# A Strassen up-projection, with the gated channels and an embedding product through DRAM, in a one-core transformer layer

## The chip, the core and the metric

The kernel runs on one core of a Trainium2 chip. The metric is the device time of one execution in microseconds (us): the median of three runs.

## What is computed

One decoder layer on 512 tokens of width 2048, all in 32-bit floats: input norm and projection, two groups of mixing heads, an output projection, and then the part that the change touches:

```python
h = h + rms_norm(mixed, ln_mix_post[l])
y = conv_gated_mlp(rms_norm(h, ln_ffn_pre[l]), w_up[l], conv_w[l], conv_b[l], w_down[l])
h = h + rms_norm(y, ln_ffn_post[l])
h = h + (p[l] @ w_pe[l]) * jax.nn.sigmoid(h @ w_pg[l])

def conv_gated_mlp(u, w_up, conv_w, conv_b, w_down):
    up = u @ w_up
    pad = jnp.pad(up, ((0, 0), (CONV_WIDTH - 1, 0), (0, 0)))
    up = conv_b + sum(pad[:, j:j + S] * conv_w[j] for j in range(CONV_WIDTH))
    gate, val = jnp.split(up, 2, axis=-1)
    return (jax.nn.gelu(gate, approximate=True) * val) @ w_down
```

w_up is 2048 x 11264 (5632 gate and 5632 value channels), w_down 5632 x 2048, w_pg 2048 x 2048, w_pe 256 x 2048; the convolution has three taps along the tokens.

## The kernel before, in words

**Matmuls.** Each 32-bit operand is split exactly into two parts of a shorter float type, a high part `hi` (a cast on ScalarE, ACT) and a low part `lo` (a subtraction on VectorE, DVE), and a product is three matmuls: hi by hi, hi by the activations' low part, lo by hi. The inner dimension of 2048 is 16 blocks (`kb`) of 128. `project_cols` (lines 148 to 150) has the weights stationary and gives channels by tokens; `project_rows` (lines 165 to 167) has the activations stationary and gives tokens by columns. Weights come as 1-MB loads that SyncE (SP) issues into two tiles `raw` (line 120), and are split in halves of 128x1024 (lines 132 and 133) into four `hi` and four `lo` tiles, which each come free when the matmuls that read them have ended. The same split of activations is lines 178 and 179 (`split_to`).

**Order.** A scheduler of the framework fixes the order of every engine's instructions when the program is built; pieces of code have priorities (`PRI_W` for weights, `PRI_E` for evictions), and generators in a list `steps` are run a step at a time between the matmuls. Nothing is reordered when the program runs: an instruction that waits holds up all that stand behind it on its engine or DMA queue.

**Stages.** After the mixing heads and the output projection (`ps_wo`), `residual` (lines 645 to 684) takes two of the four 128-token tiles at a time: x is loaded in 256-KB pieces `xp` on ACT's queue through two tiles (line 652), added (653), the result `y` is squared and summed for the norm (657, 658), written to `h_dram` from GpSimd's queue (POOL, 660), scaled (667), transposed on TensorE (PE, 679) and split into the activations u2T. While the second half of the tokens goes through this, the first 256 channels of gate and of value are projected for the first half of the tokens (`ps_ue`, matmuls of 256 columns).

Then the MLP runs over 22 pairs of channel blocks of 128. `up_gate` (736) projects a pair of gate blocks with matmuls of 512 tokens (`ps_ug`), `up_val` (747) the value blocks (`ps_uv`). The convolution is an ACT instruction with scale and bias (726) and two DVE instructions (727, 728); gelu is 743, gate by value 755, and the product is split into gT. After every second pair, `down` (767) multiplies the four blocks of gT before with 512 rows of w_down (`ps_dn`) and adds into `yacc` (763, 765). The last two groups of four blocks (`ps_dl`) are left for the tail, where the norm and residual (`finish`, 786 to 806), the transposes of h (815), the gate product (`ps_pg`) and the embedding product of p (`ps_pe`) follow, and `gate_out` (855 to 858) writes the output.

## Time and profile before

| | us |
|---|---|
| runs | 2604.68 median (2603.14 to 2606.24) |
| profiled execution | span 2600.5, from the first to the last instruction |
| PE busy | 2560.4 (98%) |
| DVE busy | 1255.1 (48%) |
| ACT busy | 903.0 (35%) |
| POOL busy | 118.0 (5%) |
| mean granted clock of PE | 0.998 of full speed |

Of the profiled execution the span alone is known; the runs' median is 4.2 us above it. A row of the profile has its line in the kernel, engine, operation, and output<-inputs by the names in the code, without buffer numbers. Matmuls overlap, so the distance between starts tells what one costs.

### The profile page before, as it was taken

The numbers are of one execution on the slowest core, as the hardware profiler recorded it, in microseconds if no ns is written. First come the engines' busy times: TensorE is split into PE (matmuls) and PEld (weight loads), VectorE is DVE, ScalarE is ACT, GpSimd is POOL, SyncE is SP. The second block draws the span as 40 slices with busy tenths as digits, with TensorE's granted clock in tenths as the row PEclk, the third lists the DMA queues.
The fourth block names the chain that finished last, engine by engine and source line by source line (L and its number), as shares of the span: only waits on it lengthen the run. The fifth ranks groups of instructions, "written<-read, shape, count | busy, mean of one in ns | idle before, by whom it ended". The sixth has DMA issues, their size and how long they took to land.

```text
span 2600.5 us, 28630 instructions
## 1 busy us (share of the span) xinstructions
PE 2560.4 (98%) x11821; PEld 2131.2 (82%) x11821; DVE 1255.1 (48%) x1772; ACT 903.0 (35%) x1244; POOL 118.0 (5%) x123
## 2 busy tenths in 40 slices
PE   7999999999999999999999999999999999999999
PEld 6888888888888788888888888888888888887787
DVE  5467377344453674244444444444444444368533
ACT  4454355233343553332323232323232323344321
POOL 1101011000000000000000000000000000004000
PEclk9999999999999999999999999999999999999999
DMA  5222222322343763332223222222222232256522
GB/s 198 87 86 80 89 85 86 110 90 89 98 146 118 242 207 113 98 98 97 97 97 98 97 97 97 98 97 97 98 98 97 97 97 97 97 197 191 170 97 81
DMA packets 211550, 293.36 MB, mean 113 GB/s; under 512 B 5612, under 2 KB 141788, under 8 KB 210396
## 3 DMA queue, kind: packets, MB, share of 16 engines
q1 hardware_dynamic: 206460, 276.33, 32.4%
q0 software_dynamic: 2656, 11.01, 1.1%
q10 hardware_dynamic: 2304, 4.20, 0.5%
q8 instruction: 93, 1.52, 0.2%
q14 instruction: 37, 0.30, 0.0%
HBM read 279.45 MB, written 12.06 MB: 112 GB/s over the span
## 4 chain that ended last, share of the span: by engine, by line
PE 93%; DMA 3%; DVE 2%; ACT 1%; issue 1%; POOL 0%; SPq 0%; ACTq 0%; POOLq 0%; DVEq 0%
PE ps_ug L150 6%; PE ps_uv L149 6%; PE ps_uv L150 6%; PE ps_ug L149 6%; PE ps_ug L148 6%; PE ps_uv L148 6%; PE ps_dn L165 5%; PE ps_dn L166 5%; PE ps_dn L167 5%; PE ps_pg L165 2%; PE ps_pg L166 2%; PE ps_pg L167 2%; PE ps_wo L165 2%; PE ps_wo L166 2%; PE ps_wo L167 2%; PE ps_hf L148 1%
## 5 line engine op out<-in xcount | busy, mean ns | idle before, releaser
L150 PE MATMUL ps_uv<-u2T,lo_uv 128*128 128x512 f32 x672 | 261.6, 389 | 0.0
L149 PE MATMUL ps_uv<-u2T,hi_uv 128*128 128x512 f32 x672 | 261.6, 389 | 0.0
L148 PE MATMUL ps_ug<-u2T,hi_ug 128*128 128x512 f32 x672 | 261.6, 389 | 0.0
L148 PE MATMUL ps_uv<-u2T,hi_uv 128*128 128x512 f32 x672 | 261.6, 389 | 0.0
L150 PE MATMUL ps_ug<-u2T,lo_ug 128*128 128x512 f32 x672 | 261.6, 389 | 0.0
L149 PE MATMUL ps_ug<-u2T,hi_ug 128*128 128x512 f32 x672 | 261.6, 389 | 0.0
L133 DVE TENSOR_TENSOR lo_ug<-raw_ug,hi_ug 128x1024 fp32r<-128x1024 f32 x88 | 107.8, 1225 | 244.9 <-ACT hi_ug L132 244.8
L165 PE MATMUL ps_dn<-hi_dn,gT 128*128 128x512 f32 x576 | 224.2, 389 | 0.0
L167 PE MATMUL ps_dn<-hi_dn,gT 128*128 128x512 f32 x576 | 224.2, 389 | 0.0
L166 PE MATMUL ps_dn<-lo_dn,gT 128*128 128x512 f32 x576 | 224.2, 389 | 0.0
L133 DVE TENSOR_TENSOR lo_uv<-raw_uv,hi_uv 128x1024 fp32r<-128x1024 f32 x88 | 107.8, 1225 | 217.8 <-ACT hi_uv L132 217.7
L132 ACT CAST hi_uv<-raw_uv 128x1024 fp32r<-128x1024 f32 x88 | 92.4, 1050 | 259.5 <-PE ps_dn L167 149.7
L132 ACT CAST hi_ug<-raw_ug 128x1024 fp32r<-128x1024 f32 x88 | 92.6, 1054 | 256.2 <-PE ps_uv L149 252.0
L133 DVE TENSOR_TENSOR lo_dn<-raw_dn,hi_dn 128x1024 fp32r<-128x1024 f32 x72 | 88.2, 1225 | 168.8 <-ACT hi_dn L132 168.8
L149 PEld LDWEIGHTS ps_ug<-u2T,hi_ug 128*128 128x128 f32 x672 | 126.2, 188 | 26.1
L148 PEld LDWEIGHTS ps_uv<-u2T,hi_uv 128*128 128x128 f32 x672 | 126.2, 188 | 26.2
L149 PEld LDWEIGHTS ps_uv<-u2T,hi_uv 128*128 128x128 f32 x672 | 126.2, 188 | 26.1
L148 PEld LDWEIGHTS ps_ug<-u2T,hi_ug 128*128 128x128 f32 x672 | 126.2, 188 | 26.1
L150 PEld LDWEIGHTS ps_ug<-u2T,lo_ug 128*128 128x128 f32 x672 | 126.2, 188 | 26.1
L150 PEld LDWEIGHTS ps_uv<-u2T,lo_uv 128*128 128x128 f32 x672 | 126.2, 188 | 26.1
L132 ACT CAST hi_dn<-raw_dn 128x1024 fp32r<-128x1024 f32 x72 | 75.6, 1050 | 195.9 <-PE ps_dn L167 117.2
L167 PEld LDWEIGHTS ps_dn<-hi_dn,gT 128*128 128x128 f32 x576 | 108.2, 188 | 22.5
(315 smaller groups left out, 5250.4 us busy)
## 6 DMA issues: line engine op xcount, KB each, us to landing
raw_ug<-in_w_up SPq DMA_DIRECT2D x44, 1024.0 KB, 5.0
raw_uv<-in_w_up SPq DMA_DIRECT2D x44, 1024.0 KB, 5.0
raw_dn<-in_w_down SPq DMA_DIRECT2D x36, 1024.0 KB, 5.0
raw_wo<-in_w_out SPq DMA_DIRECT2D x24, 1024.0 KB, 5.1
raw_pg<-in_w_pg SPq DMA_DIRECT2D x20, 1024.0 KB, 5.3
raw_dl<-in_w_down SPq DMA_DIRECT2D x16, 1024.0 KB, 5.1
raw_hi<-in_w_in SPq DMA_DIRECT2D x8, 1024.0 KB, 5.7
raw_hq<-in_w_in SPq DMA_DIRECT2D x8, 1024.0 KB, 5.1
```

The costliest lines, as they stand in the source:

```text
L132: nc.scalar.copy(hi, raw[:, k0 : k0 + step, :])
L133: nc.vector.tensor_tensor(lo, raw[:, k0 : k0 + step, :], hi.bitcast(F32), op=ALU.subtract)
L148: nc.tensor.matmul(o, hi[:, i, cols], ah, start=kb == 0, stop=False)
L149: nc.tensor.matmul(o, hi[:, i, cols], al, start=False, stop=False)
L150: nc.tensor.matmul(o, lo[:, i, cols], ah, start=False, stop=kb == KB - 1)
L165: nc.tensor.matmul(ps[t], ah[:, cols], hi[:, i, :], start=kb == 0, stop=False)
L166: nc.tensor.matmul(ps[t], ah[:, cols], lo[:, i, :], start=False, stop=False)
L167: nc.tensor.matmul(ps[t], al[:, cols], hi[:, i, :], start=False, stop=kb == nkb - 1)
```

## The change

The up-projection is done block by block of 128 gate and 128 value channels, 44 in all. The inner dimension is halved (8 blocks of 128), the tokens are halved (256) and gate and value are the two halves of the channels: a product of 2 x 2 by 2 x 2 blocks, which seven products of sums of halves give in place of eight. `ua[1]` to `ua[7]` are the sums of activation halves, made once; the sums of weight halves (lines 798, 799, 800, 804) are made for each block, and each operand is split (`split_pair`, ACT line 638, DVE line 639). A product is 24 matmuls of 256 columns (813 to 815). Three PSUM tiles per block collect the products; copies on ACT (820, 855) and additions on DVE (835, 846, 852) take the partial results between products. Convolution, gelu and product are lines 863 to 869, and the gated block is written to `g_dram` by POOL (870). Weights come as four 512-KB loads per block (783), whose rows have 512 bytes, into tiles of `rawp` and, for odd blocks, of the MLP's own pool `ml`.

The embedding product of p moves from the tail to the place between output projection and MLP; its 16 tiles of 128x512 `pv` are copied by ACT (765) into the two tiles that `xp` also uses and written to `pe_dram` by POOL (766); `gate_out` loads them again (992). The write of h_dram is issued by ACT (687). The down-projection follows when all blocks are done: gated blocks are loaded from g_dram (901), split, and multiplied in three parts of 24, 12 and 8 blocks. Its pool `fin` takes the memory of `ml`, so the loads of `lno_b` (893) and of the first gated blocks wait for ml's last reader, the last write to g_dram. Tiles for squares that nobody reads become bfloat16, and the scratch of GpSimd's DMAs is set to 8192.

```diff
+    g_dram = tc.dram_tile([NFB, P, S], F32, name="g_dram")
+    pe_dram = tc.dram_tile([S, D], F32, name="pe_dram")
...
+    def split_pair(pool, src, ncol, name):
+        hi = splitp.tile([P, H8, ncol], F32R, tag="hi", name=f"hi_{name}")
+        lo = splitp.tile([P, H8, ncol], F32R, tag="lo", name=f"lo_{name}")
+        nc.scalar.copy(hi, src)
+        nc.vector.tensor_tensor(lo, src, hi.bitcast(F32), op=ALU.subtract)
+        return hi, lo
...
+        def turn_half(src, dst, t, name):
+            for c in range(2):
+                ps = aux.tile([P, 4, P], F32, tag="aux", name=f"{name}{c}")
+                for i in range(4):
+                    nc.tensor.transpose(ps[:, i, :], src[:, (c * 4 + i) * P : (c * 4 + i + 1) * P], ident)
+                r = slice(c * 4, c * 4 + 4)
+                split_to(dst[:, r, 0, half[t % 2]], dst[:, r, 1, half[t % 2]], ps)
...
+                nc.scalar.dma_start(h_dram[t * P : (t + 1) * P, :], y[t])
                 nc.vector.tensor_reduce(st[t][:, 2:3], sq[t][:, 4:8], axis=mybir.AxisListType.X, op=ALU.add)
                 power(st[t][:, 3:4], st[t][:, 2:3], 1, D)
-                nc.gpsimd.dma_start(h_dram[t * P : (t + 1) * P, :], y[t])
...
+        def second_half():
+            yield from residual((2, 3))
+            for t in (2, 3):
+                scale(t, (2, 3, 0, 1))
+            for t in (2, 3):
+                turn_half(y[t][:, k2], ua[3], t, f"u3t{t}")
+                nc.vector.tensor_tensor(y[t - 2][:, k1], y[t - 2][:, k1], y[t][:, k1], op=ALU.subtract)
+                nc.vector.tensor_tensor(y[t][:, k1], y[t][:, k2], y[t][:, k1], op=ALU.subtract)
+                turn_half(y[t - 2][:, k1], ua[5], t, f"u5t{t}")
+                nc.vector.scalar_tensor_tensor(
+                    y[t][:, k2], y[t - 2][:, k1], -1.0, y[t][:, k2], op0=ALU.mult, op1=ALU.subtract
+                )
+                turn_half(y[t][:, k2], ua[6], t, f"u6t{t}")
+                nc.vector.scalar_tensor_tensor(
+                    y[t - 2][:, k2], y[t][:, k2], -1.0, y[t - 2][:, k2], op0=ALU.mult, op1=ALU.subtract
+                )
+                yield
...
+            for t in (2, 3):
+                turn_half(y[t][:, k1], ua[7], t, f"u7t{t}")
+            for t in (2, 3):
+                turn_half(y[t - 2][:, k2], ua[4], t, f"u4t{t}")
...
-        steps.append(residual((2, 3)))
+        pT = act_slot("A1", "pT")
...
+        p_act = slot_view([pT], 4)
+        for n in range(4):
+            pe = project_rows(w_pe[0], 0, n * S, 2, p_act, full, acc, f"pe{n}", unit=2)
+            for t in range(TT):
+                with tc.high_priority(PRI_E):
+                    pv = wo.tile([P, S], F32, tag="xp", bufs=2, name=f"pv{t}_{n}")
+                    nc.scalar.copy(pv, pe[t])
+                    nc.gpsimd.dma_start(pe_dram[t * P : (t + 1) * P, cut[n]], pv)
+        ua[3], ua[5] = b_slot(0, "ua3", 256), b_slot(1, "ua5", 256)
+        ua[6], ua[7] = act_slot("A0", "ua6", 256), act_slot("A1", "ua7", 256)
+        ua[4] = a4p.tile([P, H8, 2, 256], F32R, name="ua4")
+        steps.append(second_half())
...
-        early = {}
-        for c0 in (0, DFF):
-            early[c0] = project_cols(
-                w_up[0], c0, 2, slot_view(u2T, 4), acc, f"ue{c0}", tok=slice(0, 2 * P),
-                pri=PRI_W if c0 == 0 else 1,
-            )
...
+        def load_group(j):
+            raws = []
+            for k in range(2):
+                r = (ml if j % 2 else rawp).tile([P, H8, 2, P], F32, tag="raw", bufs=2, name=f"raw_u{j}_{k}")
+                for i, c in enumerate((j * P, DFF + j * P)):
+                    nc.sync.dma_start(
+                        r[:, :, i, :],
+                        w_up[0, k * H8 * P : (k + 1) * H8 * P, c : c + P].rearrange("(k p) n -> p k n", p=P),
+                    )
+                raws.append(r)
+            return raws
...
+        def operands(j):
+            r1, r2 = load_group(j)
+            w11, w12, w21, w22 = r1[:, :, 0, :], r1[:, :, 1, :], r2[:, :, 0, :], r2[:, :, 1, :]
+            s5 = ml.tile([P, H8, P], F32, tag="s5", name=f"s5_{j}")
+            ops = {}
+            with tc.high_priority(PRI_W):
+                ops[1] = split_pair(ml, w11, P, f"u{j}_1")
+                ops[2] = split_pair(ml, w21, P, f"u{j}_2")
+                nc.vector.tensor_tensor(s5, w12, w22, op=ALU.add)
+                nc.vector.tensor_tensor(w12, w11, w12, op=ALU.add)
+                nc.vector.tensor_tensor(w11, s5, w11, op=ALU.add)
+                ops[6] = split_pair(ml, w11, P, f"u{j}_6")
+                ops[5] = split_pair(ml, s5, P, f"u{j}_5")
+                ops[7] = split_pair(ml, w12, P, f"u{j}_7")
+                nc.vector.tensor_tensor(w21, w21, w11, op=ALU.add)
+                ops[3] = split_pair(ml, w21, P, f"u{j}_3")
+                ops[4] = split_pair(ml, w22, P, f"u{j}_4")
+            return ops
...
+        def product(o, ops, i, first):
+            hi, lo = ops[i]
+            for kb in range(H8):
+                ah, al = ua[i][:, kb, 0, :], ua[i][:, kb, 1, :]
+                nc.tensor.matmul(o, hi[:, kb, :], ah, start=first and kb == 0, stop=False, skip_group_check=True)
+                nc.tensor.matmul(o, hi[:, kb, :], al, start=False, stop=False, skip_group_check=True)
+                nc.tensor.matmul(o, lo[:, kb, :], ah, start=False, stop=kb == H8 - 1, skip_group_check=True)
...
+            def begin(self):
+                product(self.a, self.ops, 1, True)
+                self.x = partial(self.a, f"xx{self.j}")
+                product(self.b, self.ops, 2, True)
+                with tc.high_priority(PRI_E):
+                    nc.vector.tensor_tensor(self.cu[0][:, :HT], self.x, self.b, op=ALU.add)
...
+            def middle(self):
+                j = self.j
+                self.c = acc.tile([P, S], F32, tag="acc", name=f"psc_{j}")[:, :HT]
+                product(self.a, self.ops, 6, False)
+                u2 = partial(self.a, f"ub{j}")
+                product(self.c, self.ops, 5, True)
+                product(self.a, self.ops, 7, False)
+                u3 = partial(self.a, f"uc{j}")
+                with tc.high_priority(PRI_E):
+                    nc.vector.tensor_tensor(self.cu[1][:, HT:], u3, self.c, op=ALU.add)
+                self.u2 = u2
+            def end(self):
+                product(self.c, self.ops, 3, False)
+                with tc.high_priority(PRI_E):
+                    nc.vector.tensor_tensor(self.cu[0][:, HT:], self.u2, self.c, op=ALU.add)
+                product(self.a, self.ops, 4, False)
+                with tc.high_priority(PRI_E):
+                    nc.scalar.copy(self.cu[1][:, :HT], self.a)
...
+                nc.vector.scalar_tensor_tensor(t[1], t[1], -1.0, t[0], op0=ALU.mult, op1=ALU.mult)
+                nc.gpsimd.dma_start(g_dram[j], t[1])
...
+        now = Group(0)
+        now.begin()
+        for j in range(NFB):
+            if j + 1 < NFB:
+                nxt = Group(j + 1)
+            if j == 0:
+                nxt.begin()
+            now.middle()
+            if 0 < j < NFB - 1:
+                nxt.begin()
+            now.end()
+            now.gate()
+            now = nxt
...
-        def up_val(pr, gates):
-            ps = up(DFF, pr, f"uv{pr}")
-            g = pr // 2
-            if pr % 2 == 0:
-                gT[g] = act_slot(f"A{g % 2}", f"gT{g}")
...
+        def load_gated(q, tag):
+            gt = homes[tag[0]](tag, f"gT{q}")
+            for c in range(2):
+                gs = fin.tile([P, 2, S], F32, tag="gs", bufs=2, name=f"gs{q}_{c}")
+                nc.sync.dma_start(gs, g_dram[q * 4 + c * 2 : q * 4 + c * 2 + 2].rearrange("b p t -> p b t"))
+                r = slice(c * 2, c * 2 + 2)
+                split_to(gt[:, r, 0, :], gt[:, r, 1, :], gs)
+            return gt
...
-        for pr in range(NFB // 2):
-            gates = up_gate(pr)
-            if pr % 2 == 0 and 2 <= pr < NFB // 2 - 2:
-                down(pr // 2 - 1)
-            up_val(pr, gates)
...
+        parts = (
+            (range(0, 6), ("A2", "A3", "B0", "B1", "A1", "A0")),
+            (range(6, 9), ("A2", "A3", "B0")),
+            (range(9, 11), ("A1", "A0")),
+        )
...
+        gts = [load_gated(q, tag) for q, tag in zip(*parts[0])]
+        for part, (qs, tags) in enumerate(parts[:2]):
+            ahead = []
+            for n in range(4):
+                ps = project_rows(
+                    w_down[0], qs[0] * 512, n * 512, len(qs) * 4, slot_view(gts, 4), full,
+                    (acc, aux)[n % 2], f"dn{part}_{n}", tag=("acc", "aux")[n % 2],
+                )
+                for t in range(TT):
+                    accumulate(ps[t], t, n, part)
+            nqs, ntags = parts[part + 1]
+            gts = [load_gated(q, tag) for q, tag in zip(nqs, ntags)]
...
+                pv = fin.tile([P, S], F32, tag="pv", bufs=3, name=f"pv{t}_{n}")
+                nc.sync.dma_start(pv, pe_dram[t * P : (t + 1) * P, nn])
```

**Order of DVE.** A stretch in the middle of the MLP. Before (splits of the weights of value pair 8 and gate pair 9, lo_uv and lo_ug, with sums of the down-projection into yacc between them):

```order
L133 TENSOR_TENSOR lo_uv8_1_0_10576<-raw_uv8_1_10573,hi_uv8_1_0_10575 128x1024
L765 TENSOR_TENSOR yacc_7227<-yacc_7227,ps_dn3_3_0_10447 128x512
L765 TENSOR_TENSOR yacc_7227<-yacc_7227,ps_dn3_3_1_10448 128x512
L765 TENSOR_TENSOR yacc_7227<-yacc_7227,ps_dn3_3_2_10449 128x512
L765 TENSOR_TENSOR yacc_7227<-yacc_7227,ps_dn3_3_3_10450 128x512
L133 TENSOR_TENSOR lo_uv8_1_4_10604<-raw_uv8_1_10573,hi_uv8_1_4_10603 128x1024
L133 TENSOR_TENSOR lo_ug9_0_0_10651<-raw_ug9_0_10648,hi_ug9_0_0_10650 128x1024
L133 TENSOR_TENSOR lo_ug9_0_4_10679<-raw_ug9_0_10648,hi_ug9_0_4_10678 128x1024
L133 TENSOR_TENSOR lo_ug9_1_0_10709<-raw_ug9_1_10706,hi_ug9_1_0_10708 128x1024
```

Now (in `lo_u38_6` 38 is the block and 6 the product; rows that write raw or s5 are sums of weights; cv36 is the end of block 36's convolution and gate, cu37_1 a partial result of block 37):

```order
L639 TENSOR_TENSOR lo_u37_4_15823<-raw_u37_1_15790,hi_u37_4_15822 128x1024
L865 SCALAR_TENSOR_TENSOR cv36_1_16014<-cu36_1_15594,cols_c_90,cv36_1_16014 128x510
L869 SCALAR_TENSOR_TENSOR cv36_1_16014<-cv36_1_16014,cv36_0_16009 128x512
L639 TENSOR_TENSOR lo_u38_1_16028<-raw_u38_0_16020,hi_u38_1_16027 128x1024
L800 TENSOR_TENSOR raw_u38_0_16020<-s5_38_16026,raw_u38_0_16020 128x8x128
L639 TENSOR_TENSOR lo_u38_2_16032<-raw_u38_1_16023,hi_u38_2_16031 128x1024
L798 TENSOR_TENSOR s5_39_16259<-raw_u39_0_16253,raw_u39_1_16256 128x1024
L804 TENSOR_TENSOR raw_u38_1_16023<-raw_u38_1_16023,raw_u38_0_16020 128x8x128
L639 TENSOR_TENSOR lo_u38_6_16039<-raw_u38_0_16020,hi_u38_6_16038 128x1024
L799 TENSOR_TENSOR raw_u39_0_16253<-raw_u39_0_16253 128x8x128
L846 TENSOR_TENSOR cu37_1_15827<-uc37_16138,psc_37_16063 128x256
```

Where weight splits and sums of results alternated, line 846 now stands behind three splits and four sums of weights; it is the last reader of the PSUM tile psc_37 before product 3 of block 37 adds to that tile.

**Order of ACT.** Its instructions and the DMAs of its queue ahead of the second half of the tokens (xp2_2 is the third of the four pieces of token tile 2; jh are squares, jk those of the output projection). Before:

```order
L652 DMA xp2_2_6877<-in_x 128x512
L657 ACTIVATE jh2_0_6870,sq2_5881<-y2_5877 128x512
L132 CAST hi_ue5632_0_0_7109<-raw_ue5632_0_7107 128x1024
L657 ACTIVATE jh2_1_6875,sq2_5881<-y2_5877 128x512
L652 DMA xp2_3_6882<-in_x 128x512
L132 CAST hi_ue5632_0_4_7137<-raw_ue5632_0_7107 128x1024
L657 ACTIVATE jh2_2_6880,sq2_5881<-y2_5877 128x512
L652 DMA xp3_0_6891<-in_x 128x512
L132 CAST hi_ue5632_1_0_7167<-raw_ue5632_1_7165 128x1024
```

Now:

```order
L765 COPY pv2_3_7079<-ps_pe3_2_7037 128x512
L765 COPY pv3_3_7082<-ps_pe3_3_7038 128x512
L681 DMA xp2_0_7096<-in_x 128x512
L681 DMA xp2_1_7101<-in_x 128x512
L686 ACTIVATE jh2_0_7099,sq2_5886<-y2_5882 128x512
L681 DMA xp2_2_7106<-in_x 128x512
L686 ACTIVATE jh2_1_7104,sq2_5886<-y2_5882 128x512
L681 DMA xp2_3_7111<-in_x 128x512
L686 ACTIVATE jh2_2_7109,sq2_5886<-y2_5882 128x512
```

The x loads of tiles 2 and 3, of which the first two had been issued earlier, now all stand behind the last of the 16 pv copies, and no weight casts stand between them.

**Order of SP.** Its DMAs where the up-projection ends. Before:

```order
L120 DMA raw_uv21_0_15248<-in_w_up 128x8x256
L120 DMA raw_uv21_1_15306<-in_w_up 128x8x256
L120 DMA raw_dl0_9_0_0_15390<-in_w_down 128x4x512
L120 DMA raw_dl0_9_1_0_15428<-in_w_down 128x4x512
L120 DMA raw_dl0_9_2_0_15466<-in_w_down 128x4x512
L120 DMA raw_dl0_9_3_0_15504<-in_w_down 128x4x512
```

Now:

```order
L783 DMA raw_u43_0_17185<-in_w_up 128x8x128 x2
L783 DMA raw_u43_1_17188<-in_w_up 128x8x128 x2
L122 DMA raw_dn0_0_0_17626<-in_w_down 128x4x512
L122 DMA raw_dn0_0_1_17684<-in_w_down 128x4x512
L122 DMA raw_dn0_0_2_17742<-in_w_down 128x4x512
L122 DMA raw_dn0_0_3_17800<-in_w_down 128x4x512
L893 DMA lno_b_17566<-in_ln_ffn_post 128x2048
L901 DMA gs0_0_17569<-g_dram_71 128x2x512
L901 DMA gs0_1_17573<-g_dram_71 128x2x512
```

Down-projection weights followed the last up weights; now the 1-MB row lno_b and then the first gated blocks stand between them and the first down product.

## Rows read from the trace of the kernel before

**Rows 1.** page, busy time of the engines (share of the span, instructions)

```profile
PE 2560.4 (98%) x11821; PEld 2131.2 (82%) x11821; DVE 1255.1 (48%) x1772; ACT 903.0 (35%) x1244; POOL 118.0 (5%) x123
```

**Rows 2.** page, the chain that ended last, by engine

```profile
PE 93%; DMA 3%; DVE 2%; ACT 1%; issue 1%; POOL 0%; SPq 0%; ACTq 0%; POOLq 0%; DVEq 0%
```

**Rows 3.** windows: us, then busy of PE, PEld, DVE, ACT, POOL, clock, DMA share, GB/s

```profile
928.20:984.40 56.20, 51.65 (x419) 51.05 (x418) 39.56 (x52) 31.26 (x48) 5.88 (x10) 0.97 0.66 220
984.40:2334.00 1349.60, 1349.60 (x5956) 1118.15 (x5956) 585.93 (x660) 389.50 (x450) 0.00 (x0) 1.00 0.31 102
2334.00:2600.50 266.50, 252.77 (x1128) 206.53 (x1126) 131.57 (x151) 87.77 (x124) 40.38 (x36) 0.98 0.42 137
2419.90:2423.80 3.90, 3.90 (x10) 3.12 (x10) 1.75 (x3) 0.53 (x2) 0.00 (x0) 0.50 0.81 267
```

**Rows 4.** timeline of PE (start us, us): first and last of 97 starts

```profile
1009.66 0.39 PE L148 MATMUL ps_uv<-u2T,hi_uv 128*128 128x512 f32 x1
...
1031.42 0.39 PE L148 MATMUL ps_ug<-u2T,hi_ug 128*128 128x512 f32 x1
```

**Rows 5.** timeline of PE: first and last of 59 starts

```profile
966.00 0.28 PE L150 MATMUL ps_ue<-u2T,lo_ug 128*128 128x256 f32 x1
...
972.95 0.28 PE L148 MATMUL ps_ue<-u2T,hi_uv 128*128 128x256 f32 x1
```

**Rows 6.** matmuls by line and shape | busy us, mean ns | idle before

```profile
L148 PE MATMUL ps_ug<-u2T,hi_ug 128*128 128x512 f32 x672 | 261.6, 389 | 0.0
...
L150 PE MATMUL ps_ue<-u2T,lo_ue 128*128 128x256 f32 x64 | 18.1, 283 | 0.0
```

**Rows 7.** ACT and DVE by line and shape | busy us, mean ns | idle before

```profile
L132 ACT CAST hi_ug<-raw_ug 128x1024 fp32r<-128x1024 f32 x88 | 92.6, 1054 | 256.2 <-PE ps_uv L149 252.0 <-PE ps_ue L149 2.8 <-DMA raw_ug<-in_w_up 1.4
...
L726 ACT ACTIVATE cg<-ps_ug,cols_c 128x512 f32<-128x512 f32 x42 | 32.7, 777 | 38.9 <-PE ps_ug L150 38.9
...
L763 ACT COPY yacc<-ps_dn 128x512 f32<-128x512 f32 x16 | 9.4, 586 | 7.4 <-PE ps_dn L167 7.4
...
L391 DVE TENSOR_TENSOR m_zq<-m_zq,q 128x256 f32<-128x256 f32 x16 | 6.7, 416 | 0.0
```

**Rows 8.** tile out: the DMAs of 256 KB that write it

```profile
L858 POOL DMA_DIRECT2D out<-sg x12: 539/539/620, 2428.8 to 2548.4; - x12
...
DMA to landing us min/median/max: 2.3/3.2/6.4
```

**Rows 9.** tile xp: its 16 loads of 256 KB

```profile
DMA to landing us min/median/max: 3.7/5.9/6.5
```

**Rows 10.** timeline of DVE, four instructions in a row

```profile
949.03 0.68 DVE L179 TENSOR_TENSOR u2T<-u2t,u2T 128x512 fp32r<-128x512 f32 x1
949.63 1.22 DVE L133 TENSOR_TENSOR lo_ug<-raw_ug,hi_ug 128x1024 fp32r<-128x1024 f32 x1
950.76 0.74 DVE L653 SCALAR_TENSOR_TENSOR y<-y,st,xp 128x512 f32<-128x512 f32 x1
951.43 1.22 DVE L133 TENSOR_TENSOR lo_ug<-raw_ug,hi_ug 128x1024 fp32r<-128x1024 f32 x1
```

**Rows 11.** page, DMA issues: count, KB each, median us to landing

```profile
raw_ug<-in_w_up SPq DMA_DIRECT2D x44, 1024.0 KB, 5.0
...
raw_dn<-in_w_down SPq DMA_DIRECT2D x36, 1024.0 KB, 5.0
```

**Rows 12.** windows, columns as in rows 3

```profile
1530.00:1545.00 15.00, 15.00 (x68) 12.43 (x67) 5.08 (x5) 3.62 (x5) 0.00 (x0) 1.00 0.35 114
```

**Rows 13.** chain that ended last, in order of time: start, us, what

```profile
2345.03 7.88 DMA raw_dl<-in_w_down
...
2409.07 4.93 DMA raw_pg<-in_w_pg
```

**Rows 14.** waits from 920 to 990 us: in total, times, longest

```profile
DVE y L653 <- DMA xp<-in_x: 5.8, 2, 3.3
```

More of the change, by code (lines that the diff above doesn't have):

```diff
@@ new lines, in first_half @@
+        def first_half():
+            yield from residual((0, 1))
+            for t in (0, 1):
+                scale(t, (0, 1))
+                yield
+                turn_half(y[t][:, k1], ua[1], t, f"u1t{t}")
+                scale(t, (2, 3))
+                yield
+                turn_half(y[t][:, k2], ua[2], t, f"u2t{t}")
+        def second_half():
[11 more added lines that the diff above has]
+                turn_half(y[t][:, k2], ua[6], t, f"u6t{t}")
+                nc.vector.scalar_tensor_tensor(
+                    y[t - 2][:, k2], y[t][:, k2], -1.0, y[t - 2][:, k2], op0=ALU.mult, op1=ALU.subtract
+                )
+                yield
+            for t in (2, 3):
+                turn_half(y[t][:, k1], ua[7], t, f"u7t{t}")
+            for t in (2, 3):
+                turn_half(y[t - 2][:, k2], ua[4], t, f"u4t{t}")
@@ L693, in trunk @@
             evac(ps, (0, 1), n)
-        u2T = [act_slot("A2", "u2T0"), act_slot("A3", "u2T1"), b_slot(0, "u2T2"), b_slot(1, "u2T3")]
+        ua[1], ua[2] = act_slot("A2", "ua1", 256), act_slot("A3", "ua2", 256)
         lnf = [row(ln_ffn_pre, n, "lnf") for n in range(4)]
-        steps.append(residual((0, 1)))
+        steps.append(first_half())
         step()
@@ L703, in trunk @@
         pace[0] = 24
-        steps.append(residual((2, 3)))
-        drain()
-        early = {}
-        for c0 in (0, DFF):
-            early[c0] = project_cols(
-                w_up[0], c0, 2, slot_view(u2T, 4), acc, f"ue{c0}", tok=slice(0, 2 * P),
-                pri=PRI_W if c0 == 0 else 1,
-            )
-    u2_act = slot_view(u2T, 4)
+        pT = act_slot("A1", "pT")
+        for t in range(TT):
+            pt = wo.tile([P, 256], F32, tag="pt", name=f"pt{t}")
+            nc.sync.dma_start(pt, p[0, 0, t * P : (t + 1) * P, :])
+            ps = aux.tile([P, 4, P], F32, tag="aux", name=f"ptr{t}")
+            for i in range(2):
+                nc.tensor.transpose(ps[:, i, :], pt[:, full[i]], ident)
+            split_to(pT[:, 0:2, 0, full[t]], pT[:, 0:2, 1, full[t]], ps[:, 0:2, :])
@@ new lines, in trunk, with accumulate @@
+    with tc.tile_pool(name="fin", bufs=2) as fin:
+        lno_b = fin.tile([P, D], F32, bufs=1, name="lno_b")
+        nc.sync.dma_start(lno_b, ln_ffn_post[0:1, :].partition_broadcast(P))
+        homes = {"A": act_slot, "B": lambda tag, name: b_slot(int(tag[1:]), name)}
+        def load_gated(q, tag):
[6 more added lines that the diff above has]
+            return gt
+        def accumulate(ps, t, n, part):
@@ L760, in accumulate @@
             nn = slice(n * 512, (n + 1) * 512)
             with tc.high_priority(PRI_E):
-                if g == 0:
+                if part == 0:
                     nc.scalar.copy(yacc[:, t, nn], ps)
@@ L765, in accumulate @@
                     nc.vector.tensor_tensor(yacc[:, t, nn], yacc[:, t, nn], ps, op=ALU.add)
-        def down(g):
-            for n in range(4):
-                ps = project_rows(
-                    w_down[0], g * 512, n * 512, 4, slot_view([gT[g]], 4), full, aux, f"dn{g}_{n}", tag="aux"
-                )
-                for t in range(TT):
-                    accumulate(ps[t], t, n, g)
-        for pr in range(NFB // 2):
-            gates = up_gate(pr)
-            if pr % 2 == 0 and 2 <= pr < NFB // 2 - 2:
-                down(pr // 2 - 1)
-            up_val(pr, gates)
-    with tc.tile_pool(name="fin", bufs=2) as fin:
-        lno_b = fin.tile([P, D], F32, bufs=1, name="lno_b")
-        nc.sync.dma_start(lno_b, ln_ffn_post[0:1, :].partition_broadcast(P))
+        parts = (
[3 more added lines that the diff above has]
+        )
         def finish(t):
@@ L827, in trunk @@
                 pace[0] = 12
-            for g in (NG - 2, NG - 1):
+            for g in range(2):
                 for n in range(4):
                     ps = project_rows(
-                        w_down[0], g * 512, n * 512, 4, slot_view([gT[g]], 4),
+                        w_down[0], (q0 + g) * 512, n * 512, 4, slot_view([gts[g]], 4),
                         full[th * 2 : th * 2 + 2], aux, f"dl{th}_{g}_{n}", tag="aux",
```

124 lines of the change are left out of this document (49 added, 75 removed).

## The prediction

> **What bounds the kernel now.** I read first the busy times [rows 1] and the chain that ended last [rows 2]: TensorE is busy 98% of the span and carries 93% of the chain, VectorE half of it. Then the windows [rows 3]: from 984.40 to 2334.00 us, where the up-projection and most of the down-projection run, PE has no idle time at all; what idle time there is lies in the stage before (928.20 to 984.40) and in the last 266.50 us. So in the middle only the number of matmuls and the spacing of their starts count, and any new wait is a loss. Last I read the spacing: 96 steps of 512 columns from 1009.66 to 1031.42 [rows 4] give 21.76/96 = 0.2267 us; 58 steps of 256 columns from 966.00 to 972.95 [rows 5] give 6.95/58 = 0.1198 us, of which I use 0.1199. The mean durations, 389 and 283 ns [rows 6], overlap their neighbours and must not be summed.
>
> **Products of the up-projection.** Before, each of 44 channel blocks takes 16 x 3 matmuls of 512 columns for the gate and as many for the value, 96 in all. Now it takes 7 x 8 x 3 = 168 of 256 columns. 96 x 0.2267 = 21.76 us against 168 x 0.1199 = 20.14 us: 1.62 us less, and 44 times that is **-71.3 us**. Of the same kind: 384 half-width products of the first pair, which stood in place of 192 full ones, are gone (46.0 against 43.5 us, **-2.5**). One column in eight is saved, 2.72 us a block; 1.1 us of that goes to the shorter matmuls, whose start-up each pays.
>
> **Head, between the output projection and the first product 6.** Call T the end of the last output-projection matmul (928.2 us before). Before, the next 56.2 us hold 46.0 us of useful products, so 10.2 us are lost. Now 96 matmuls of the embedding product (moved from the tail, 21.8 us, no net cost) and products 1 and 2 of block 0 (5.8 us) are all that can run until the second half's operands stand. What paces it is a pair of 256-KB tiles: the 16 evictions pv and the 8 residual loads xp share them, and on ACT's queue the xp loads stand behind the last pv copy (the order extract of ACT). One use of a tile by pv is a copy, 0.59 us [rows 7], and a write that lands after 2.3, 3.2 or 6.4 us [rows 8]; with 3.2 and 0.1 for the semaphores a pair takes 3.9 us. The first copy comes at T+6.9 (transposes and first 24 products of pT, whose slot the output projection holds until T), so eight pairs end at T+38; with 2.3 it is T+31, with 6.4 T+64. Then 8 loads pass through two tiles, in about 5 serial trips of load and scaling. In before these loads landed after 3.7 to 6.5 us [rows 9] beside weight loads; alone I take 3.0, between 2.3 (the quickest 256-KB write) and 3.7, and with 0.67 for the scaling and the square behind it the last row of y stands at **T+60**. The VectorE chain behind it is 8 scalings at 0.67, 20 splits at 0.60 and 8 sums of 128x1024 at 1.14 (starts of [rows 10]): 5.4 + 12.0 + 9.1 = 26.5, with the small reductions ahead 28. Before there were only 8 splits and no sums. Product 6 so starts near **T+88**. 88 - 27.6 = 60.4 us are lost in place of 10.2: **+50.2**. Blocks 0 and 1 have no product in front of them to hide their splits and loads: **+5** more, chosen from two casts of 1.05 [rows 7] and two 1.13 splits [rows 10].
>
> **One block in the steady state.** PE runs, after product 6 of a block, its 5 and 7, then 1 and 2 of the next, 13 steps of 4, then 3. Product 3 adds to a PSUM tile that line 846 on VectorE must have read: it is due 4 x 2.88 + 13 x 0.12 = 13.08 us after product 6 ended. On VectorE line 846 stands behind the split of product 2's weights, lines 798 and 804, the split for product 6 and line 799 (the order extract of DVE). The split for 2 waits for the tile that product 7 gives back at 5.76, and for its cast: 5.76 + 0.1 + 1.05 + 1.14 = 8.05; four operations of 1.14 make 12.6, line 846 0.42 [rows 7] and the semaphores 13.1 to 13.4. So PE waits 0 to 0.3 us in every block, and the rest of VectorE (7 splits, 4 sums, 3 small sums, 4 convolution steps, 1 product: 17 us of 20.14) and ACT (about 11 us) fit beside it. A second loop ends at the same place: line 798 needs the block after next's weights, whose load is released by the split for product 4. From line 846 through 3, the rest of 4, product 6, the cast and split for 4, the load and five VectorE operations back to line 846 it is 14.5 us and the load X. With X = 5.65 it just fills 20.14. Before, a 1-MB load landed in 5.0 us whether its rows had 1 KB or 2 KB [rows 11]; the issue of a second descriptor list adds 0.4, so X = 5.4 and nothing is lost. The rows now have 512 bytes, which no row here shows. If the packet and not the byte set the time, the data part (1.05 MB at 114/0.35 = 325 GB/s [rows 12], 3.2 us) doubles: X = 8.6, 2.9 us a block. I stay near the value that two row sizes agree on and take 0.3 us a block for both loops: **+13.2**; bounds 0 and 2.9 a block. The Trainium skill (DMA: Bandwidth & Descriptors, Specifications) gives 512 B as the smallest transfer at line rate; by it the term would be that of the first loop alone, 0 to 13. No run here has shown it.
>
> **From up to down.** Before, down-projections stood among the up-projections and no one waited. Now all blocks go through g_dram. The last block's second half has no other products beside it (**+1.7**). Then copy 0.4, bias 0.78 [rows 7], two convolution steps 1.34, product 0.6, write 2.3 to 3.2, then on SP lno_b, 1 MB, ahead of the first two gated blocks (the extract of SP), 6.6 us for 1.5 MB at 325 GB/s with 1.8 of latency, a cast 1.05: 16 us idle, and 2 for the half clock that follows: after the idle time near 2411 to 2420 PE was granted 0.50 for 3.9 us [rows 3], which is 1.2 GHz. **+18**. Bounds 14 and 24. The write of h_dram, now on ACT's queue, has nobody waiting. The tail loses its embedding products, keeps its late loads [rows 13] and gets 16 loads of 256 KB on SP, which have a column of gate products (43 us) as cover and would cost VectorE a few us without it: 0, plus or minus 5.
>
> **Sum.** -71.3 - 2.5 + 50.2 + 5 + 1.7 + 18 + 13.2 = +14.3 us. The profiled execution has a span of 2600.5 us; the median, 2604.68, is 4.2 above it. The change lands near **2619 us**.
>
> **Rivals.**
> 1. *The shared tiles turn round quickly, and it is faster.* The place is pv and xp in the head. With writes and loads both at 2.3 the head is 7.2 + 3.5 us shorter; with line 846 in time as well (no 13.2) the sum is -9.6: **2595 us**. It decides below 3.1 us a pv pair. For it: the 2.3 in [rows 8] was reached beside weight loads, and line 846 is due within 0.3 us. Against it: the median is 3.2, and loads of x took 3.7 or more and made VectorE wait 5.8 us in this very stage [rows 14].
> 2. *The next weights land late.* Each us of X over 5.65 costs 44 us. At X = 6.7, one us a block, it is **2650 us**. For it: 512-byte rows and a g_dram write of 256 KB beside them. Against it: 102 GB/s is a third of what the queues can move [rows 3, 12].
> 3. *Even.* The step times and head as summed, no wait at line 846 (sum +1): **2606 us**.
> 4. *A narrow matmul costs only its columns.* At 2.4 GHz 512 columns are 213.3 ns and 256 are 106.7, so both spacings hold 13 ns beside the columns. Were these not paid in the new stream, a block would save 96 x 0.2133 - 168 x 0.1067 = 2.56 us, 0.94 more: 41 us less, **2578 us**. Against it: the 13 ns are there at both widths [rows 4, 5]. The Trainium skill (TensorE: Matmul & The Clock Gate, Back-to-back issue gap) gives N/2.4 + 2.5 ns for a warm gap, 215.8 and 109.2; by it a block would save 2.38 us and the kernel come out near 2586 us. The trace's 226.7 and 119.8 speak against it.
> 5. *The narrow matmuls keep their 283 ns.* By the mean durations [rows 6] a block would cost 47.5 instead of 37.3 us and the kernel over 400 us more. The starts in [rows 5] exclude it.
>
> **How the numbers follow.** A measurement of this kernel tells about 0.2%, 5.2 us, from no change. Forecast (+5 to +35): 0.43. Even: 0.17. Rival 1: 0.26. Rival 2 beyond +35: 0.11. Rival 4: 0.03, rival 5 and what else could fail: nothing that I can price. So faster 0.29, same 0.17, slower 0.54. As cases of both signs hold much, the forecast's own range is 2610 to 2640; 8 in 10 is 2590 to 2655, from the low ends of the head without a wait at line 846 to a load one us late.
>
> **What would show it.** Starts of products 0.120 us apart; PE idle 50 us and more between T and the first product 6, with pv copies 3 to 4 us apart in pairs; the first product 3 matmul of a block waiting 0 to 0.5 us for VectorE line 846; some 16 us without PE work ahead of the down-projection, with clock 0.5 behind it. Wrong would be: steady blocks that take over 21 us or end before 20.1, a wait for raw_u at line 798, or a head under 75 us.

## The result, and the profile after

The changed kernel takes 2636.67 us (median of 4, 2630.56 to 2639.82) against 2603.91 for the kernel before in the same comparison: a ratio of 1.0123, 95% interval 1.0108 to 1.0138. It is slower by 32.8 us, where the forecast had 14.3: the sign was right, and 2636.7 lies in the range of 2590 to 2655. The profiled execution took 2638.69 us with a span of 2636.9, 36.4 above the span before. Of the versions tried below, the one with the embedding product back in the tail had one execution of 2967.2 us at a mean granted clock of 0.79, which is left out of its time.

Windows of the changed kernel, cut where its stages end (columns as in rows 3): from the last matmul of the output projection to the first product 6, from there to the last product of the up-projection, to the first matmul of the down-projection, to the end; then a stretch in the middle, and product 6 of block 0.

```profile
929.60:1020.00 90.40, 47.82 (x235) 37.41 (x232) 45.79 (x66) 34.36 (x68) 12.15 (x24) 0.77 0.43 139
1020.00:1939.90 919.90, 896.67 (x7344) 887.29 (x7344) 757.22 (x828) 455.27 (x613) 23.31 (x43) 0.99 0.40 114
1939.90:1955.80 15.90, 0.13 (x2) 0.00 (x0) 5.49 (x8) 4.06 (x6) 0.54 (x1) 0.57 0.63 223
1955.80:2636.90 681.10, 666.95 (x2944) 550.00 (x2944) 277.03 (x278) 204.96 (x242) 40.74 (x36) 0.99 0.42 139
...
1100.00:1800.00 700.00, 683.72 (x5615) 676.86 (x5615) 579.68 (x635) 345.42 (x466) 17.84 (x33) 1.00 0.40 112
1020.60:1026.40 5.80, 4.65 (x22) 4.65 (x22) 5.63 (x5) 2.15 (x3) 0.00 (x0) 0.50 0.60 159
```

Against [rows 3] the reader sees where PE's idle time now lies: between 1020 and 1939.9 PE was busy in 896.67 of 919.90 us, where the corresponding stretch before had none idle. The term to watch is the 919.9 us of the second window: its 7344 matmuls at 0.1199 us need 880.5, so 39.4 us are lost there, and the forecast had 19.9 (5 for the first blocks, 13.2 for the steady state, 1.7 for the last block).

What PE waited for, from 1020 to 1956 us (in total, times, longest):

```profile
PE psc L813 <- DVE cu L846: 18.0, 28, 2.2
PE ps_dn L167 <- ACT gT L180: 15.8, 1, 15.8
PE psa L813 <- ACT hi_u L638: 3.9, 2, 2.9
PE psa L813 <- ACT uc L820: 1.3, 1, 1.3
PE psa L815 <- DVE lo_u L639: 1.3, 1, 1.3
PE psa L813 <- ACT ub L820: 1.2, 1, 1.2
```

What VectorE waited for, from 1045 to 1915 us:

```profile
DVE s L798 <- DMA raw_u<-in_w_up: 20.5, 30, 2.2
```

The place is the one that the forecast named: product 3 (`psc`) waits for line 846, and line 798 ahead of it waits for the weights. The rows show one block of it, on VectorE:

```profile
1303.46 1.22 DVE L639 TENSOR_TENSOR lo_u<-raw_u,hi_u 128x1024 fp32r<-128x1024 f32 x1
...
1309.16 1.23 DVE L639 TENSOR_TENSOR lo_u<-raw_u,hi_u 128x1024 fp32r<-128x1024 f32 x1 [0.39 <-ACT hi_u L638]
1310.92 1.23 DVE L798 TENSOR_TENSOR s<-raw_u,raw_u 128x1024 f32<-128x1024 f32 x1 [0.53 <-DMA raw_u<-in_w_up]
1312.06 1.22 DVE L804 TENSOR_TENSOR raw_u<-raw_u,raw_u 128x1024 f32<-128x1024 f32 x1
1313.19 1.22 DVE L639 TENSOR_TENSOR lo_u<-raw_u,hi_u 128x1024 fp32r<-128x1024 f32 x1
1314.33 1.22 DVE L799 TENSOR_TENSOR raw_u<-raw_u 128x1024 f32<-128x1024 f32 x1
1315.47 0.41 DVE L846 TENSOR_TENSOR cu<-uc,psc 128x256 f32<-128x256 f32 x1
```

and on PE, where 17 steps of 256 columns from 1313.16 to 1315.20 are 0.120 us each, as [rows 5] had it:

```profile
1313.16 0.28 PE L814 MATMUL psb<-ua,hi_u 128*128 128x256 f32 x1
...
1315.20 0.28 PE L813 MATMUL psa<-ua,hi_u 128*128 128x256 f32 x1
1315.93 0.39 PE L813 MATMUL psc<-ua,hi_u 128*128 128x256 f32 x1 [0.46 <-DVE cu L846]
1316.16 0.28 PE L814 MATMUL psc<-ua,hi_u 128*128 128x256 f32 x1
```

The split for product 4 (1303.46, over at 1304.68) gives the raw tile back, and line 798 starts at 1310.92, the moment the next weights are there: the load X of the forecast (from the end of that split to the landing of the weights that line 798 reads) is 6.24 us here, not 5.4. In the mean of 40 blocks line 798 starts 6.23 us after that split ends, and in none under 5.7. The split for product 2 had ended 0.5 us before; without that wait line 846 would have been in time to within 0.1 us. From line 846 to line 846 a block takes 20.9 us in the mean of 40 in the middle, where 168 steps are 20.14. The list has only 18.0 us of waits for line 846, since a matmul's recorded 0.28 us overlaps the next start and short waits are not listed. By the distances between starts, product 3's first matmuls come 24.9 us too late in all, and the steps behind them are another 5.2 too long (1315.93 to 1316.16 is one): 30.1 us.

### The profile page after: what moved, and what is told of

The parts are those of the page before. It is cut to its first block, busy times and chain, and to the rows that moved or that the text cites. A ratio compares the mean times of both kernels' runs of the same rounds, so it can differ in the third digit from the quotient of the medians.

```text
span 2636.9 us, 35933 instructions
## 1 busy us (share of the span) xinstructions
PE 2521.5 (96%) x14845; PEld 2232.9 (85%) x14845; DVE 1582.6 (60%) x2091; ACT 1091.6 (41%) x1550; POOL 140.2 (5%) x179
## 3 DMA queue, kind: packets, MB, share of 16 engines
q10 hardware_dynamic: 2880, 8.39, 0.9%
## 5 line engine op out<-in xcount | busy, mean ns | idle before, releaser
L638 ACT CAST hi_u<-raw_u 128x1024 fp32r<-128x1024 f32 x264 | 276.2, 1047 | 394.5 <-PE psc L814 216.8
L813 PE MATMUL psa<-ua,hi_u 128*128 128x256 f32 x1408 | 400.3, 284 | 6.9 <-ACT hi_u L638 3.9
L815 PE MATMUL psa<-ua,lo_u 128*128 128x256 f32 x1408 | 400.2, 284 | 1.3 <-DVE lo_u L639 1.3
L814 PE MATMUL psa<-ua,hi_u 128*128 128x256 f32 x1408 | 400.0, 284 | 0.0
L639 DVE TENSOR_TENSOR lo_u<-raw_u,hi_u 128x1024 fp32r<-128x1024 f32 x264 | 322.5, 1222 | 57.6 <-ACT hi_u L638 52.2
L813 PEld LDWEIGHTS psa<-ua,hi_u 128*128 128x128 f32 x1408 | 271.8, 193 | 8.2 <-ACT hi_u L638 4.3
L815 PEld LDWEIGHTS psa<-ua,lo_u 128*128 128x128 f32 x1408 | 272.0, 193 | 1.5 <-DVE lo_u L639 1.5
L814 PEld LDWEIGHTS psa<-ua,hi_u 128*128 128x128 f32 x1408 | 271.9, 193 | 0.0
L167 PE MATMUL ps_dn<-hi_dn,gT 128*128 128x512 f32 x576 | 225.0, 391 | 15.8 <-ACT gT L180 15.8
L813 PE MATMUL psc<-ua,hi_u 128*128 128x256 f32 x704 | 204.2, 290 | 18.4 <-DVE cu L846 18.0
L815 PE MATMUL psc<-ua,lo_u 128*128 128x256 f32 x704 | 200.0, 284 | 0.0
L814 PE MATMUL psc<-ua,hi_u 128*128 128x256 f32 x704 | 199.8, 284 | 0.0
L813 PEld LDWEIGHTS psc<-ua,hi_u 128*128 128x128 f32 x704 | 135.4, 192 | 26.7 <-DVE cu L846 26.7
L814 PEld LDWEIGHTS psc<-ua,hi_u 128*128 128x128 f32 x704 | 135.7, 193 | 0.0
L815 PEld LDWEIGHTS psc<-ua,lo_u 128*128 128x128 f32 x704 | 135.6, 193 | 0.0
```

The lines of the kernel that those rows point to most:

```text
L167: nc.tensor.matmul(ps[t], ah[:, cols], hi[:, i, :], start=kb == 0, stop=False)
L638: nc.scalar.copy(hi, src)
L639: nc.vector.tensor_tensor(lo, src, hi.bitcast(F32), op=ALU.subtract)
L813: nc.tensor.matmul(o, hi[:, kb, :], ah, start=first and kb == 0, stop=False, skip_group_check=True)
L814: nc.tensor.matmul(o, hi[:, kb, :], al, start=False, stop=False, skip_group_check=True)
L815: nc.tensor.matmul(o, lo[:, kb, :], ah, start=False, stop=kb == H8 - 1, skip_group_check=True)
```

## The experiments

The ratios are to the kernel before in the same session. That kernel took 2603.6 us in the session of the first runs, 2600.7 in that of the three edits together and of the two versions with the embedding product in the tail, and 2602.3 in that of the two loads, so a difference from the changed kernel holds to about 3 us.

**Line 846 ahead of the weight sums.**

```diff
-                with tc.high_priority(PRI_E):
+                with tc.high_priority(2 * PRI_W):
                     nc.vector.tensor_tensor(self.cu[1][:, HT:], u3, self.c, op=ALU.add)
```

> Edit: line 846 gets a priority above the sums and splits of weights, so that VectorE does it right after the split for product 2; nothing else. Theory 1 (line 846 ties product 3 to the sums and through line 798 to the weights' landing): PE's wait for line 846, 18.0 us in the changed kernel, falls under 2, a block takes 20.2 to 20.3 us in place of 20.8, and the time falls by 20 to 30 us, to 2607 to 2617. Rival (VectorE is too full or the weights too late wherever line 846 stands): the wait moves to products 5, 6 or 7 and the time falls by less than 8 us.

Measured: 2607.37 us, 29.3 below the changed kernel, ratio to the kernel before 1.0015 (1.0006 to 1.0025). PE's wait for line 846 is gone from its list, and a block takes 20.16 us. In its window from the first product 6 to the last product, 888.9 us, 8.4 are above the 880.5 that the matmuls need:

```profile
1017.60:1906.50 888.90, 883.98 (x7344) 882.95 (x7344) 764.11 (x828) 456.28 (x613) 23.29 (x43) 1.00 0.41 117
```

VectorE has the same 828 instructions to do, so it was the order on it, not its work, that held PE. Line 798 still waits for weights now and then (3.7 us in all), and nobody behind it is in a hurry. The 8.4 us are the first blocks and the last, for which the forecast had 6.7; the steady blocks of the change so lost 39.4 - 8.4 = 31 us, not 13.2.

**Weight rows of 1 KB.**

```diff
-                for i, c in enumerate((j * P, DFF + j * P)):
-                    nc.sync.dma_start(
-                        r[:, :, i, :],
-                        w_up[0, k * H8 * P : (k + 1) * H8 * P, c : c + P].rearrange("(k p) n -> p k n", p=P),
-                    )
+                nc.sync.dma_start(
+                    r.rearrange("p k i n -> p k (i n)"),
+                    w_up[0, k * H8 * P : (k + 1) * H8 * P, j * 2 * P : (j + 1) * 2 * P].rearrange("(k p) n -> p k n", p=P),
+                )
```

> Edit: the two 512-KB loads with 512-byte rows become one 1-MB load with 1-KB rows; it takes 256 neighbouring columns of the weights in place of 128 gate and 128 value channels, so other products are computed, of the same size. Theory 1 (the load, after the split for product 4, lands too late because short rows take longer): line 798's wait for the weights, 20.5 us, falls under 5, a block takes 20.2 to 20.4 us, the time falls by 12 to 20 us. Rival (VectorE's chain ahead of line 846 is by itself too long): line 798's wait goes, a block stays at 20.7 to 20.8 and the time within 5 us.

Measured: 2612.06 us, 24.6 below the changed kernel, ratio 1.0034 (1.0021 to 1.0048); more than expected. A block takes 20.44 us in the mean, most of them 20.25, and line 798 waits in 5 blocks in place of 30, 5.7 us in all, a little over the 5 of theory 1. Where it does not wait it starts 5.62 us after the split for product 4, close to the forecast's break-even of 5.65. With the order unchanged, VectorE's own chain so costs 0.1 us in an ordinary block, the low part of the forecast's 0 to 0.3; the rest of the loss was the load. The window and the wait, lines counted from this kernel:

```profile
1100.00:1800.00 700.00, 694.73 (x5747) 692.51 (x5746) 589.05 (x650) 354.43 (x479) 18.37 (x34) 1.00 0.35 116
```

```profile
DVE s L797 <- DMA raw_u<-in_w_up: 5.7, 5, 2.9
```

**Two loads with rows of 1 KB.** The run before changed the length of the rows and the number of loads at once; this one keeps two loads; its lines stand in place of the same ones.

```diff
+                for i in range(2):
+                    r0 = (k * H8 + i * 4) * P
+                    nc.sync.dma_start(
+                        r[:, i * 4 : i * 4 + 4].rearrange("p k i n -> p k (i n)"),
+                        w_up[0, r0 : r0 + 4 * P, j * 2 * P : (j + 1) * 2 * P].rearrange("(k p) n -> p k n", p=P),
+                    )
```

> Edit: as the run with 1-KB rows, but in two 512-KB loads of four 128-row blocks each, so that the number of loads and their size are those of the change and only the rows differ (again 256 neighbouring columns, other weights). Theory 1 (the row length sets how long a load takes): a block takes 20.4 to 20.5 us as with one load, line 798 waits under 8 us in all, the time is 2608 to 2616. Rival (two loads behind one another, not their rows, cost the time): a block stays at 20.7 to 20.9 and the time above 2625.

Measured: 2625.6 us, ratio 1.0083 (1.0057 to 1.0109), between the two. Theory 1's numbers miss; the rival's are just met. But the mean of 20.73 us is no longer that of an ordinary block: half of the blocks take 20.24 to 20.31 us (in the change 3 of 43 are under 20.4), and line 799, this kernel's line 798, waits in 15 (the window and the wait):

```profile
1100.00:1800.00 700.00, 687.22 (x5661) 683.66 (x5660) 582.46 (x642) 350.08 (x472) 18.44 (x34) 1.00 0.35 115
```

```profile
DVE s L799 <- DMA raw_u<-in_w_up: 15.6, 15, 2.7
```

So neither theory holds alone: the row length makes every block late by a little, and two loads in place of one make some blocks late by more. Of the 24.6 us, about 11 go with the rows; the other 13.5 go only with one load in place of two. Why about every third block is late with two loads is left open: in some of those blocks SP's second issue itself took 1.1 to 1.4 us in place of 0.5, in others not. The write to g_dram, which GpSimd issues in every block while these loads are under way, stands in all three versions, and no run tells what it costs them.

**The embedding evictions out of the x tiles.**

```diff
+        pvs = act_slot("A0", "pvs")
...
-                    pv = wo.tile([P, S], F32, tag="xp", bufs=2, name=f"pv{t}_{n}")
+                    pv = pvs[:, t, n % 2, :].bitcast(F32)
```

> Edit: the 16 pv evictions go to eight places in slot A0, which is free then, and no longer share two tiles with the x loads. Theory 1 (the pair of tiles paces the head): the last row of y stands 35 to 45 us after the output projection in place of 62, the first product 6 starts at 60 to 70 in place of 90, and the time falls by 20 to 30 us. Rival (VectorE's chain of splits and sums, or the queue of POOL with its writes ahead of the norm's power, paces it): product 6 starts after 80 us or later and the time falls by less than 10.

Measured: 2613.47 us, 23.2 below the changed kernel, ratio 1.0043 (1.0026 to 1.0061). The last residual row is written at 968.9, 39.6 us after the output projection (62.3 in the change), and product 6 starts after 66.1 us (90.3). Timeline of VectorE, the last addition of x, and of PE, the first product 6:

```profile
968.16 0.75 DVE L682 SCALAR_TENSOR_TENSOR y<-y,st,xp 128x512 f32<-128x512 f32 x1
```

```profile
995.46 0.38 PE L814 MATMUL psa<-ua,hi_u 128*128 128x256 f32 x1 [2.88 <-ACT hi_u L638]
995.68 0.28 PE L815 MATMUL psa<-ua,hi_u 128*128 128x256 f32 x1
997.25 0.58 PE L816 MATMUL psa<-ua,lo_u 128*128 128x256 f32 x1 [1.29 <-DVE lo_u L639]
997.62 0.42 PE L814 MATMUL psa<-ua,hi_u 128*128 128x256 f32 x1
```

The 27 us from y to product 6 stay nearly as they were (28.0 in the change): VectorE's chain of scalings, splits and sums of the activations and, at its end, block 0's own weight sums, since what product 6 waits for is the cast of one of them. The steady blocks are nearly as slow as in the change (20.78 us).

**The embedding product back in the tail.** pT, the product and `gate_out` are again as before:

```diff
-            pe = project_rows(w_pe[0], 0, n * S, 2, p_act, full, acc, f"pe{n}", unit=2)
...
-                    nc.gpsimd.dma_start(pe_dram[t * P : (t + 1) * P, cut[n]], pv)
...
+            pe = project_rows(w_pe[0], 0, n * S, 2, p_act, full, aux, f"pe{n}", tag="aux", unit=2)
...
-                    nc.vector.tensor_tensor(sg, sg, pv, op=ALU.mult)
+                    nc.vector.tensor_tensor(sg, sg, pe[t], op=ALU.mult)
```

> Edit: the embedding product goes back to the tail, as in the kernel before, without pe_dram; all else of the change stays. Theory 1 (the loss of the head lies in the pv evictions that share two tiles with x): the x loads run at once, y stands near 20 us after the output projection and product 6 starts at 48 to 55 us in place of 90; 21.8 us of products are back in the tail, so the time falls by 14 to 21 us, to 2616 to 2623. Rival (the five extra operands alone make the head long, with or without the embedding product): product 6 after 65 us, time within 5 us of the changed kernel or slower.

Measured: 2609.83 us, ratio 1.0032 (1.0020 to 1.0044): 26.8 below the changed kernel, 6 more than expected, of which 3 can be the session. y stands 18.9 us after the output projection and product 6 starts after 46.7. So 43.6 us of head go and 21.8 us of products come back in the tail, 21.8 net; the blocks were 0.2 us quicker in the profiled execution besides. From y to product 6 it is 27.8 us, so the five extra operands do not need a head of 90 us.

**lno_b behind the gated blocks.**

```diff
-        nc.sync.dma_start(lno_b, ln_ffn_post[0:1, :].partition_broadcast(P))
...
         gts = [load_gated(q, tag) for q, tag in zip(*parts[0])]
+        nc.sync.dma_start(lno_b, ln_ffn_post[0:1, :].partition_broadcast(P))
```

> Edit: the 1-MB row lno_b is loaded after the first part's gated blocks in place of before them. Theory 1 (lno_b's megabyte stands ahead of the first gated blocks): PE's idle time ahead of the down-projection falls from 15.8 us to 12 to 13. Rival (the write to g_dram and the release of ml's memory set it): it stays at 15 or more.

Measured, in one execution of 2632.27 us: PE's wait ahead of the down-projection falls from 15.8 us to 13.5, less than theory 1 said and more than the rival allowed. The megabyte costs 2.3 us there. The rest is the last block's own chain and its way through DRAM: 5.6 us from the last product to the end of line 869, 0.3 to the issue of the write, 2.8 from there to the issue of the loads at 1942.98, 3.8 until the first has landed and 1.0 for the cast.

```profile
PE ps_dn L167 <- ACT gT L180: 13.5, 1, 13.5
...
1940.16 0.54 POOL L870 DMA_DIRECT2D g_dram<-cv  x1 [15.11 <-DVE cv L869]
1946.78 1.04 ACT L180 CAST gT<-gs 128x1024 fp32r<-128x1024 f32 x1 [8.49 <-DMA gs<-g_dram]
```

**The three edits together.**

> Edit: line 846 ahead of the sums, pv in slot A0, and lno_b behind the gated blocks, together. Theory 1 (three separate losses, one in each stage): they add up, -29 - 23 - 2 to 4 us from the changed kernel's 2636.7, that is 2580 to 2585, faster than the kernel before by 0.7 to 0.9%; a block takes 20.16 us and the first product 6 starts 66 us after the output projection. Rival (an earlier head or a quicker block runs into the next limit, the landing of weights or ACT): 2590 or more.

Measured: 2582.49 us (2578.6 to 2585.23), ratio to the kernel before 0.9926 (0.9914 to 0.9939). The losses add up: 54.2 us from the changed kernel, where 29.3 + 23.2 + 2.3 make 54.8 (by the ratios 51.3, where the three make 51.2). This version is 18 us below the kernel before. Its head and its up-projection:

```profile
928.10:994.90 66.80, 46.10 (x234) 38.52 (x232) 46.15 (x66) 33.04 (x68) 12.16 (x24) 0.84 0.56 183
994.90:1884.30 889.40, 884.80 (x7344) 883.63 (x7344) 763.93 (x828) 455.62 (x613) 23.29 (x43) 1.00 0.40 117
```

**The embedding product in the tail, with two of the edits.** "The run before" is here the one with the embedding product back in the tail.

> Edit: as the run before, with line 846 ahead of the sums and lno_b behind the gated blocks. Theory 1: it is 29 + 3 us below the run before, 2584 to 2591, and within 6 us of the version with pv in slot A0, since there the embedding product fills a head that waits anyway, and here it costs its 21.8 us in the tail. Rival (the embedding product ahead of the MLP is worth its full 21.8 us once pv has its own memory): this one is 15 to 22 us slower than that version.

Measured: 2585.24 us, ratio 0.9941 (0.9925 to 0.9956), 2.8 us above the three edits together, where theory 1 had under 6; the two intervals overlap, so which of the two is faster is not shown. It is 24.6 us below the run with the embedding product in the tail alone, not 32. The place of the embedding product is worth next to nothing, once its evictions do not stand in the way of x: in the head it makes product 6 20 us later (66.8 against 46.8), in the tail it costs its 21.8 (the tail is 22.9 longer).

## Why the prediction was wrong

Each term against the profiled executions, in us:

| step | forecast | measured | from |
|---|---|---|---|
| products | -73.8 | about -73 | 0.120 a step, as in rows 5 |
| head, lost time in place of 10.2 | +50.2 | +52.5 | 90.3 - 27.6 - 10.2 |
| first blocks and last block | +6.7 | +8.4 | the run with line 846 first |
| steady blocks | +13.2 | +31 | 39.4 - 8.4 |
| from up to down | +18 | +17.6 | 15.9 idle, 1.7 of half clock |
| tail, lost time in place of 27.5 | 0 | -1 | 681.1 - 652.9 - 1.7 - 27.5 |
| start of the stage | 0 | +1.4 | 929.6 in place of 928.2 |
| sum | +14.3 | +37 | span +36.4 |

In the tail's row 652.9 is 2880 products at 0.2267, and 27.5 is what the kernel before lost from 984.4 to its end: 1616.1, less 913.9 for 42 blocks, 652.9, and 21.8 for the embedding product.

**The step that failed** is the size of one term: "so X = 5.4 and nothing is lost", and from it "take 0.3 us a block for both loops". The loop itself was right: the wait at line 798 stood on record as a sign that the forecast is wrong, and it came, in 30 blocks. The loop breaks even at X = 5.65, and each us above costs 44. Measured, X is 6.24 in the block shown and 6.23 in the mean; 0.58 x 44 = 26 us, and with 0.1 a block for VectorE's own chain, 4 us, that is the 31 us found. Two things were in it. X was put near the value on which rows of 1 and 2 KB agree [rows 11], and rows of 512 bytes are not like these: at full use the queues move 112/0.40 = 280 GB/s in the change, 116/0.35 = 331 with 1-KB rows, and 325 by [rows 12]. For a megabyte that is 3.7 us in place of 3.2. And the second load stood in X with the 0.4 us of its issue; by the runs two loads cost about 13.5 us more in all than one, from blocks that are late by up to 2.7 us, and how that comes about is open. Two sizes that agree were read as a flat curve, and the term sat 0.25 us from its break-even, with the bound of 8.6 on record. The Trainium skill (DMA: Bandwidth & Descriptors, Specifications) gives 512 B as the smallest transfer at line rate, which pointed the same wrong way. By that rule the term would be the first loop's alone, 4 us by the run with 1-KB rows; the measurement decides against it.

The loss needs both halves of the loop, the late weights and line 846 behind line 798: the run that moves line 846 takes away all of it, the run with 1-KB rows in one load most of it.

**Rival 2**, the late weights, came a little over half way: X passed 5.65 by 0.58 us, not by the 1.05 that it took, at the price that it named.

**What held.** The spacing of 256-column matmuls (0.120) and the saving of the products, against the mean durations (rival 5) and against columns alone (rival 4). The head: the pair of tiles paced it, with y at 62.3 us (60 forecast) and product 6 at 90.3 (88). From 930 to 1020 us ACT's copies waited for the pv writes, and VectorE for the x loads behind them; the landing is that of the 16 writes, and the last three rows are the end of the head on VectorE, ACT and PE:

```profile
ACT pv L765 <- DMA pe_dram<-pv: 17.8, 12, 3.7
DVE y L682 <- DMA xp<-in_x: 18.5, 5, 14.8
DMA to landing us min/median/max: 2.6/2.7/5.9
...
1017.61 1.22 DVE L800 TENSOR_TENSOR raw_u<-s,raw_u 128x1024 f32<-128x1024 f32 x1
1018.86 1.04 ACT L638 CAST hi_u<-raw_u 128x1024 fp32r<-128x1024 f32 x1 [3.83 <-DVE raw_u L800]
1019.96 0.39 PE L813 MATMUL psa<-ua,hi_u 128*128 128x256 f32 x1 [2.87 <-ACT hi_u L638]
```

That the sums agree within 3 us is in part luck. A pair of pv writes took 4.6 us in the mean, not 3.9, since five of the first eight landed after 3.8 to 5.9 us, though the median is 2.7 and not 3.2; rival 1 needed under 3.1 a pair. The first copy and the x loads made up 3 us of it. And the 28.0 us from y to product 6 are not the forecast's chain: 17 splits, 7 sums and 4 scalings of the activations stood behind y in place of 20, 8 and 8, some 21 us, and block 0's weight sums (lines 798 to 800) and the cast behind them, which the forecast had elsewhere, made up the rest but for some waits. The runs with own memory and with the product in the tail show that the pair, not the five operands, made nearly half of the loss in the head: product 6 came 24.1 us earlier with own memory.

The move from up to down: 15.9 us idle (16 forecast), then 3.4 us in which PE was granted half its clock:

```profile
1955.80:1959.20 3.40, 3.35 (x7) 2.25 (x8) 2.44 (x2) 1.05 (x1) 0.00 (x0) 0.50 0.95 328
```

The 16 was luck too: the terms that the forecast lists before the half clock add up to 13.1 to 14.0. What they lacked is in the last block's own chain, 5.6 us from the last product to the end of line 869 in place of 3.1.

The 32.8 us of the medians are 3.6 below the profiled spans' difference; runs of the changed kernel spread over 9.3 us, those before over 3.1.

## What to carry to other kernels

Look for what stands in the order of an engine between the reader of a PSUM tile and the matmul that wants the tile back: here one priority on a 0.4-us addition was worth 29 us, more than the best load tried (24.6). Before costing a loop through a load at nothing, take the slack in us and ask whether the load's new shape can use it up; a price at two row lengths does not give the third, nor the price of one load that of two. And when two uses share a pair of tiles, cost the round trip of the longer one for every use of the other.
